# A two-layer attention encoder on one core: output shares at the handover from C to A, the turn of the output blocks, and the first load of x

## The chip, the cores and the metric

One core of a Trainium2 chip runs the whole program. The metric is the device time of one execution in microseconds (us); lower is better. The core has a matrix engine (PE, TensorE), three engines for elementwise work (DVE or VectorE, ACT or ScalarE, POOL or GpSimd), and a queue, SP, from which the transfers (DMA) are issued in order. Every engine works off its own list of instructions in order.

## What is computed

```python
for l in range(2):                                   # x: 1024 rows x 1024 features
    h = rms_norm(x, norm_g[l])
    aq, ak, av, ag, bq_lat, bkv_lat, bk_pe, bg, cq, ck, cv, cg = split_cols(h @ w_in[l])
    ya = dilated_attention(norm(aq), norm(ak), av) * silu(ag)     # 4 heads of 64
    yb = dense_attention(rope(norm(up(bq_lat))), ..., vb) * silu(bg)   # 6 heads, 96 wide
    yc = dense_attention(rope(norm(cq)), rope(norm(ck)), cv) * silu(cg)   # 6 heads, 2 for k and v
    x = x + concatenate([ya, yb, yc]) @ w_out[l]     # 256 + 384 + 384 features
```

## The kernel before, in words

Everything lies transposed: eight feature blocks of 128 partitions by 1024 positions. A matmul operand is split into a high part and a remainder, and a product takes three matmuls (high x high, high x remainder, remainder x high). `split` makes the parts: ACT writes the high part (L141), DVE or POOL the remainder (L145); `Stream` fetches weights over SP, splits them and hands them out in the order of `ws.add`. An engine given to `ws.add` fixes who makes the remainder; without one DVE and POOL take turns (`flip`).

The program begins with `WARM` 128-column matmuls on a tile of ones (L1327, each two matmul instructions of the trace). `bring` loads x chunk by chunk and prepares it (`x_prepare`: ACT L188, DVE L189; `x_square` adds up the squares, POOL L199). A layer then goes through the latent projection (L299 to L301, over k = 0..7), the v, q, kv, C and A projections, the gates (`gate(m)`, L657 to L659), six B heads and six C heads (dense), four A heads (dilated), and the output projection.

From the last four gates on, the order is a table of slots that is written by hand: `put(s, f, pri)` hangs a step on slot s, and `slots` runs them. A dense head takes 16 slots; the A heads begin around slot `base_a`. ACT keeps the order of the code; for PE, DVE, POOL and SP a scheduler sets the order from the code and the tiles' buffers. Row blocks m = 0..7 of the output take features k = 2, 3, 4 from B (`OF_B`), 5, 6, 7 from C (`OF_C`) and 0, 1 from A (`OF_A`). `EARLY[m]` says which of these are multiplied during the slots (`f_load` fetches the weights and splits them on POOL, L1087 and L1088; `f_load_x` fetches x; `f_mm` runs 9 matmuls of 512 columns for half a block, L1105 to L1107; `f_add` adds x, L1111, and stores to `x_part`), `LATE[m]` which come at the end. A block's sum lies in an S tile; there are two S tiles, and the score products (L748, L885 to L891) use them too. T tiles (four) take transposes.

An A head: score products `a_s` (L885 to L891), exponentials (L908, L910), a chain of small steps on DVE (`a_x1` to `a_x5`; `a_x4p` is a PE step, L965), then `a_norm_w` (L980) and `a_norm_c` (L984) scale the probabilities on POOL, and `a_t` transposes them on PE (L997, L1002) for the product with v (L1026). `a_end` (L1073) writes the result into the y tile of its feature block on ACT; `gate_load` (L799) loads the gate.

At the end of a layer (the output stage) `out_first` and `out_part` (L1251 to L1253) finish a block in an S tile, and `out_end` loads `x_part` (L1264), adds it (DVE L1265), stores x and, in the first layer, prepares the block for the next layer. A block that lacks only A's part is light here (12 matmuls), one that lacks C's and A's parts is heavy (30 matmuls).

## Time and profile before

| | |
|---|---|
| median of 3 runs | 1497.06 us (1496.88 to 1497.84) |
| the profiled execution | 1496.05 us, span 1494.3 us |
| PE busy | 1457.9 us (98%) |
| DVE, ACT, POOL busy | 1085.1 (73%), 895.9 (60%), 593.3 (40%) us |
| TensorE clock granted, mean | 0.991 of full |

The profile is of one execution; its own time is 1.01 us under the median, and 1.75 us of it lie outside the span. Busy time of PE includes matmuls that overlap the next one, so a PE at 100% may still run at half the clock.

### The profile page before, as it was taken

To read this page: it belongs to the slowest core of one execution; us is meant where nothing else is said; L and a number is where in the kernel's file an instruction comes from. 1 tells how busy PE (TensorE), PEld (TensorE's weight loads), DVE (VectorE), ACT (ScalarE), POOL (GpSimd) and SP (SyncE) were. 2 spreads that over 40 slices of the span, in tenths; PEclk is the share of its full clock that TensorE was granted. 3 is DMA by queue.
4 is the path that set the end of the run, shared out by engine and by line. 5 is a ranking of instruction groups with operands and counts; after the bars stand their busy time and mean duration, and the time that the engine had idled before them with its cause. 6 is when DMAs were issued, how large, how long until landed. Compare 5 with 4: busy or idle time off the path is not lost.

```text
span 1494.3 us, 23232 instructions
## 1 busy us (share of the span) xinstructions
PE 1457.9 (98%) x7928; PEld 1237.6 (83%) x7928; DVE 1085.1 (73%) x1994; ACT 895.9 (60%) x1667; POOL 593.3 (40%) x544
## 2 busy tenths in 40 slices
PE   9999999999999999899899999999999999998998
PEld 8998888788888888788679988888888888886887
DVE  6759757488889998564646497574888899985644
ACT  6572235388889997453324632343988899974531
POOL 6305421145456553553231044311354565535530
PEclk9999999999999999999999999999999999999999
DMA  7271146510342116742532621366103421157427
GB/s 229 74 249 41 51 153 200 160 57 29 91 122 57 29 43 188 202 149 80 177 131 66 242 60 50 115 208 190 57 29 79 121 69 31 43 170 208 140 72 249
DMA packets 119719, 176.01 MB, mean 118 GB/s; under 512 B 11696, under 2 KB 75568, under 8 KB 119600
## 3 DMA queue, kind: packets, MB, share of 16 engines
q1 hardware_dynamic: 119600, 174.52, 38.3%
q8 instruction: 63, 1.03, 0.3%
q14 instruction: 56, 0.46, 0.1%
HBM read 111.56 MB, written 62.91 MB: 117 GB/s over the span
## 4 chain that ended last, share of the span: by engine, by line
PE 90%; DVE 3%; issue 3%; ACT 2%; DMA 2%; POOL 1%; SPq 0%; ACTq 0%; DVEq 0%; POOLq 0%
PE S L748 15%; PE T L777 11%; PE acc L790 6%; PE acc L789 6%; PE T L658 4%; PE T L659 4%; PE T L657 4%; PE S L1105 2%; PE S L1106 2%; PE S L1107 2%; PE S L216 2%; PE S L217 2%; PE S L215 2%; PE T L693 1%; PE T L997 1%
## 5 line engine op out<-in xcount | busy, mean ns | idle before, releaser
L771 DVE TENSOR_TENSOR wl<-T,wh 128x512 fp32r<-128x512 f32 x440 | 297.6, 687 | 85.1 <-ACT wh L770 82.7
L770 ACT ACTIVATE wh<-T 128x512 fp32r<-128x512 f32 x440 | 261.1, 597 | 153.7 <-PE T L777 69.0
L764 POOL TENSOR_SCALAR u<-u,rec 128x1024 f32<-128x1024 f32 x192 | 216.8, 1129 | 272.5 <-DVE rec L763 155.2
L748 PE MATMUL S<-u,u 96*128 96x512 f32 (+1 forms) x960 | 269.2, 410 | 1.6 <-ACT u L757 1.3
L750 DVE TENSOR_REDUCE nmax<-S 128x1 f32<-128x1024 f32 x192 | 233.6, 1217 | 21.9 <-PE S L748 21.4
L777 PEld LDWEIGHTS T<-ident,u 128*128 128x128 f32 x1536 | 191.3, 140 | 50.3
L777 PE MATMUL T<-ident,u 128*128 128x128 f32 x1536 | 229.4, 272 | 0.0
L757 ACT ACTIVATE u<-S,nmax 128x1024 f32<-128x1024 f32 x192 | 213.2, 1111 | 0.3
L145 POOL TENSOR_TENSOR wl<-wr,wh 128x512 fp32r<-128x512 f32 (+2 forms) x48 | 77.6, 1619 | 318.0 <-ACT wh L141 307.2
L748 PEld LDWEIGHTS S<-u,u 96*128 96x128 f32 (+1 forms) x960 | 166.6, 189 | 29.7 <-ACT u L757 3.6
L141 ACT ACTIVATE wh<-wr 128x512 fp32r<-128x512 f32 (+2 forms) x96 | 56.8, 596 | 161.2 <-PE S L216 97.3
L657 PE MATMUL T<-u,wh 128*128 128x512 f32 x256 | 102.0, 399 | 0.0
L659 PE MATMUL T<-u,wl 128*128 128x512 f32 x256 | 100.1, 391 | 0.0
L658 PE MATMUL T<-u,wh 128*128 128x512 f32 x256 | 100.0, 391 | 0.0
L789 PE MATMUL acc<-wh,u 128*128 128x512 f32 x192 | 84.6, 441 | 0.0
L789 PE MATMUL acc<-wh,qb 128*128 128x512 f32 x192 | 82.8, 431 | 0.0
L790 PE MATMUL acc<-wl,u 128*128 128x512 f32 x192 | 75.9, 395 | 1.6 <-DVE wl L771 1.6
L790 PE MATMUL acc<-wl,qb 128*128 128x512 f32 x192 | 75.8, 395 | 0.0
L145 DVE TENSOR_TENSOR wl<-wr,wh 128x512 fp32r<-128x512 f32 (+2 forms) x48 | 42.3, 882 | 44.7 <-ACT wh L141 44.5
L1105 PE MATMUL S<-u,h 128*128 128x512 f32 x156 | 63.9, 409 | 1.6 <-DVE u L1111 1.6
L1107 PE MATMUL S<-u,h 128*128 128x512 f32 x156 | 61.7, 396 | 0.0
L1106 PE MATMUL S<-u,h 128*128 128x512 f32 x156 | 61.5, 394 | 0.0
(294 smaller groups left out, 3399.1 us busy)
## 6 DMA issues: line engine op xcount, KB each, us to landing
u<-qk_c SPq DMA_DIRECT2D x40, 256.0 KB, 4.4
wr<-in_w_g_dram SPq DMA_DIRECT2D x32, 256.0 KB, 2.6
gates<-h SPq DMA_DIRECT2D x32, 256.0 KB, 2.3
qk_c<-u SPq DMA_DIRECT2D x16, 512.0 KB, 4.0
u<-gates SPq DMA_DIRECT2D x16, 512.0 KB, 3.8
qb<-qk_a SPq DMA_DIRECT2D x32, 256.0 KB, 5.7
x_part<-u SPq DMA_DIRECT2D x16, 512.0 KB, 3.1
qb<-x_part SPq DMA_DIRECT2D x15, 512.0 KB, 4.2
```

Of the source, the lines that this page charges most:

```text
L657: T.matmul(ps[half], wh[:, w], xh[k][:, s], start=(k == 0), stop=False)
L658: T.matmul(ps[half], wh[:, w], xl[k][:, s], start=False, stop=False)
L659: T.matmul(ps[half], wl[:, w], xh[k][:, s], start=False, stop=(k == 7))
L748: T.matmul(ps[:, w], q[:, s], k[:, w], start=(i == 0), stop=(i == len(terms) - 1))
L750: V.tensor_reduce(nmax, ps, op=ALU.max, axis=AX.X, negate=True)
L757: A.activation(p, ps, AF.Exp, bias=nmax, accum_out=den)
L764: G.tensor_scalar(p, p, rec, 1.0, ALU.mult, ALU.mult)
L770: A.activation(ph, ps, AF.Copy)
L771: V.tensor_tensor(pl, ps, f32(ph), ALU.subtract)
L777: T.transpose(ps[:, i * P:(i + 1) * P], Pt[hd, 4 * half + i][0][:, j * P:(j + 1) * P], ident)
L789: T.matmul(acc, w, ph, start=(j == 0), stop=False)
L790: T.matmul(acc, w, pl, start=False, stop=(j == 7))
```

## The change

- `HALF_M`: blocks 0, 1, 3 and 5 have only B's part early, the others B's and C's. Before, blocks 0, 1 and 2 had. The four B shares stand four slots apart from `base_a - 10` on, so the last stands behind the handover; the shares of the other four blocks fill the A heads' slots (16 half blocks where 20 stood). One C share per layer, 18 matmuls, thereby goes from the A heads to the output stage.
- `f_load_x` is put three slots ahead of the block's last piece, where it was six slots ahead of its first.
- K, table and V of A's first head are put 40 and 36 slots ahead, where it was 6 to 8.
- In the output stage blocks 2 to 7 are now light, heavy, light, heavy, light, light; before heavy, then five light ones. The remainders of w_out's pieces go to DVE and POOL in turn; before those of m >= 2 went to DVE.
- `spread_r`, eight small products that spread the row norm r over the partitions (L641 to L645), is called inside `gate(0)` after k = 3; before it stood ahead of `gate(0)`.
- At the start x's chunk 0 is loaded and prepared in two halves, the first half first in SP's queue; the identity matrix goes to `load_tables`; `WARM` is 12 where it was 20; the first layer's k = 0 takes half 0 of all three row blocks ahead of half 1.

```diff
--- before.py
+++ after.py
@@ -25,8 +25,9 @@
 
 
 OF_B, OF_C, OF_A = (2, 3, 4), (5, 6, 7), (0, 1)
-EARLY = {m: ((OF_B,) if m < 3 else (OF_B, OF_C)) for m in range(8)}
-LATE = {m: ((OF_C, OF_A) if m < 3 else (OF_A,)) for m in range(8)}
+HALF_M = (0, 1, 3, 5)
+EARLY = {m: ((OF_B,) if m in HALF_M else (OF_B, OF_C)) for m in range(8)}
+LATE = {m: ((OF_C, OF_A) if m in HALF_M else (OF_A,)) for m in range(8)}
 
 
 @with_exitstack
@@ -87,7 +88,6 @@
         return ap.bitcast(F32)
 
     ident = cp.tile([P, P], F32, name="ident")
-    nc.sync.dma_start(ident, ident_in)
     ones = cp.tile([P, P], F32, name="ones")
     V.memset(ones, 1.0)
 
@@ -101,6 +101,7 @@
     sinb = cp.tile([P, NCH, 32], F32, name="sinb")
 
     def load_tables():
+        nc.sync.dma_start(ident, ident_in)
         nc.sync.dma_start(cosb, cosb_in)
         nc.sync.dma_start(sinb, sinb_in)
         nc.sync.dma_start(cosc, cosc_in)
@@ -183,10 +184,11 @@
     ws = Stream()
 
 
-    def x_prepare(k, x32, g_sb, xh, xl):
+    def x_prepare(k, x32, g_sb, xh, xl, parts=(slice(0, SEQ),)):
         hi, lo = U(F32R), U(F32R)
-        A.activation(hi, x32, AF.Copy, scale=g_sb[:, k:k + 1])
-        V.scalar_tensor_tensor(lo, x32, g_sb[:, k:k + 1], f32(hi), ALU.mult, ALU.subtract)
+        for s in parts:
+            A.activation(hi[:, s], x32[:, s], AF.Copy, scale=g_sb[:, k:k + 1])
+            V.scalar_tensor_tensor(lo[:, s], x32[:, s], g_sb[:, k:k + 1], f32(hi[:, s]), ALU.mult, ALU.subtract)
         xh.append(hi)
         xl.append(lo)
 
@@ -254,7 +256,7 @@
         g["c"] = gc
 
     state = {}
-    WARM, SK = 20, 3
+    WARM, SK = 12, 3
     MV = 2
     LS, UL = (2, 3, 4), (3, 4, 5)
     stores = []
@@ -291,14 +293,16 @@
                 load_tables()
             if k == 7:
                 make_gains2(g)
-            for m in range(3):
+            order = [(m, half) for m in range(3) for half in range(2)]
+            if k == 0 and l == 0:
+                order.sort(key=lambda e: e[1])
+            for m, half in order:
                 w = slice(m * P, m * P + P)
-                for half in range(2):
-                    o = bk[m][half]
-                    s = slice(half * 512, half * 512 + 512)
-                    T.matmul(o, wh[:, w], xh[k][:, s], start=(k == 0), stop=False)
-                    T.matmul(o, wh[:, w], xl[k][:, s], start=False, stop=False)
-                    T.matmul(o, wl[:, w], xh[k][:, s], start=False, stop=(k == 7))
+                o = bk[m][half]
+                s = slice(half * 512, half * 512 + 512)
+                T.matmul(o, wh[:, w], xh[k][:, s], start=(k == 0), stop=False)
+                T.matmul(o, wh[:, w], xl[k][:, s], start=False, stop=False)
+                T.matmul(o, wl[:, w], xh[k][:, s], start=False, stop=(k == 7))
         latr = [U() for _ in range(3)]
         for m in range(3):
             A.activation(latr[m][:, 0:512], bk[m][0], AF.Copy)
@@ -637,12 +641,14 @@
 
 
         r_bc = U()
-        ps = PS()
-        for c in range(NCH):
-            d = H()[:, :P]
-            V.tensor_scalar(d, ident, r[:, c:c + 1], None, ALU.mult)
-            T.matmul(ps[:, c * P:(c + 1) * P], ones, d, start=True, stop=True)
-        A.activation(r_bc, ps, AF.Copy)
+
+        def spread_r():
+            ps = PS()
+            for c in range(NCH):
+                d = H()[:, :P]
+                V.tensor_scalar(d, ident, r[:, c:c + 1], None, ALU.mult)
+                T.matmul(ps[:, c * P:(c + 1) * P], ones, d, start=True, stop=True)
+            A.activation(r_bc, ps, AF.Copy)
 
         last_u = []
 
@@ -658,6 +664,8 @@
                     T.matmul(ps[half], wh[:, w], xl[k][:, s], start=False, stop=False)
                     T.matmul(ps[half], wl[:, w], xh[k][:, s], start=False, stop=(k == 7))
                 run(0.8)
+                if m == 0 and k == 3:
+                    spread_r()
                 if hook is not None:
                     hook(m, k)
             for half in range(2):
@@ -1177,13 +1185,13 @@
                     put(base_a + AT0 + 8 * h + FA[1] + half, lambda h=h, half=half: fin_split(h // 2, half), 6)
         FP, FL = 6.5, 6
         rest = [(m, piece, half) for m in EARLY if len(EARLY[m]) > 1 for piece in range(2) for half in range(2)]
-        at = {(m, 0, half): base_a - 10 + 4 * m + half for m in EARLY if len(EARLY[m]) == 1 for half in range(2)}
+        at = {(m, 0, half): base_a - 10 + 4 * i + half for i, m in enumerate(HALF_M) for half in range(2)}
         at.update({u: base_a + 7 + 29 * i // len(rest) for i, u in enumerate(rest)})
         for (m, piece, half), s in at.items():
             if half == 0:
                 put(s - FL, lambda m=m, piece=piece: f_load(m, piece), 9)
-                if piece == 0:
-                    put(s - FL, lambda m=m: f_load_x(m), 9)
+                if piece == len(EARLY[m]) - 1:
+                    put(s - 3, lambda m=m: f_load_x(m), 9)
             put(s, lambda m=m, piece=piece, half=half: f_mm(m, piece, half), FP)
             if piece == len(EARLY[m]) - 1:
                 put(s + 1, lambda m=m, half=half: f_add(m, half), 6)
@@ -1205,9 +1213,10 @@
         for h in range(AH):
             s = a_slot(4 * h)
             put(s - 8, lambda h=h: q_load(qk_a, ("a", h), 0), 8)
-            put(s - 7, lambda h=h: k_load(qk_a, ("a", h), 2), 8)
-            put(s - 6, lambda h=h: a_load_tab(h), 8)
-            put(base_a + AT0 + 8 * h - 8, lambda h=h: a_load_v(h), 8)
+
+            put(s - (7 if h else 40), lambda h=h: k_load(qk_a, ("a", h), 2), 8)
+            put(s - (6 if h else 36), lambda h=h: a_load_tab(h), 8)
+            put(base_a + AT0 + 8 * h - (8 if h else 40), lambda h=h: a_load_v(h), 8)
 
         def slot(s):
             for _, _, f in sorted(at_slot.pop(s, []), key=lambda e: e[:2]):
@@ -1319,14 +1328,15 @@
         ws.hold()
         order = [(m, OF_C) for m in range(2)] + [(m, OF_A) for m in range(2)]
         for m, ks in order + [(m, ks) for m in range(2, 8) for ks in LATE[m]]:
-            ws.add(w_out[l, m, :, ks[0]:ks[-1] + 1, :], (P, len(ks), P), True, V if m >= MV else None)
+            ws.add(w_out[l, m, :, ks[0]:ks[-1] + 1, :], (P, len(ks), P), True, None)
 
 
     warm = PT()
     for _ in range(WARM):
         T.matmul(warm[:, :P], ones, ones, start=True, stop=True)
 
-    g = load_gains(0)
+    HALVES = (slice(0, 512), slice(512, SEQ))
+    g = {}
     xh, xl = [], []
     ss = QB()[:, :SEQ]
     loaded, done = [], [0]
@@ -1335,16 +1345,18 @@
         while len(loaded) < min(k + 3, 8):
             i = len(loaded)
             t = QB()[:, :SEQ]
-            nc.sync.dma_start(t, x_t[i * P:(i + 1) * P, :])
+            for j, s in enumerate(HALVES if i == 0 else (slice(0, SEQ),)):
+                nc.sync.dma_start(t[:, s], x_t[i * P:(i + 1) * P, s])
+                if i == 0 and j == 0:
+                    g.update(load_gains(0))
+                    ws.fetch(1)
             loaded.append(t)
 
     def bring(k):
-        if k == 0:
-            ws.fetch(1)
         x_load(k)
         while len(xh) < min(k + 2, 8):
             i = len(xh)
-            x_prepare(i, loaded[i], g["x"], xh, xl)
+            x_prepare(i, loaded[i], g["x"], xh, xl, HALVES if i == 0 else (slice(0, SEQ),))
         while done[0] < (k if k < 7 else 8):
             x_square(done[0], loaded[done[0]], ss)
             done[0] += 1
```

What the change moves in the engines' lists, at three places. Names end in a running number; h is a split weight of f_load, wr the raw one, qb and u operands.

PE before, the handover in the first layer: behind the last C products (L789, L790) come score products of A (L885 to L891), and among them the first transpose that needs POOL's L984 (L997).

```order
L789 MATMUL acc_6530<-wh_6681,qb_5314 128x512
L790 MATMUL acc_6530<-wl_6682,qb_5314 128x512
L885 MATMUL S_6754<-qb_6372,u_6342 128x256
L886 MATMUL S_6754<-qb_6373,u_6342 128x256
L890 MATMUL S_6754<-qb_6372,u_6345 128x256
L891 MATMUL S_6754<-qb_6373,u_6345 128x256
L885 MATMUL S_6754<-qb_6372,u_6342 128x192
L886 MATMUL S_6754<-qb_6373,u_6342 128x192
L890 MATMUL S_6754<-qb_6372,u_6345 128x256
L891 MATMUL S_6754<-qb_6373,u_6345 128x256
L885 MATMUL S_6793<-qb_6615,u_6594 128x192
L997 MATMUL T_6778<-ident,u_6329 128x128
```

The same place of PE after the change (L893 is a score product, L1113 to L1115 are f_mm):

```order
L797 MATMUL acc_6532<-wh_6682,qb_5309 128x512
L798 MATMUL acc_6532<-wl_6683,qb_5309 128x512
L1113 MATMUL S_6753<-u_3371,h_6598 128x512
L1114 MATMUL S_6753<-u_3372,h_6598 128x512
L1115 MATMUL S_6753<-u_3371,h_6599 128x512
L1113 MATMUL S_6753<-u_4066,h_6598 128x512
L1114 MATMUL S_6753<-u_4067,h_6598 128x512
L1115 MATMUL S_6753<-u_4066,h_6599 128x512
L1113 MATMUL S_6753<-u_4704,h_6598 128x512
L1114 MATMUL S_6753<-u_4705,h_6598 128x512
L1115 MATMUL S_6753<-u_4704,h_6599 128x512
L893 MATMUL S_6765<-qb_6374,u_6346 128x256
```

Nine matmuls of f_mm (the B share of block 5, first half, on tile S_6753) now follow the C products. Behind them come eight score products (the first, L893, is the last row shown), then nine more of f_mm, and only then the first transpose that needs the norms, L1005; before, nine score products alone stood ahead of it.

POOL before, the same place: the norms of the first head (L980, L984), with the split of a weight of f_load (L1087, L1088) between them.

```order
L980 TENSOR_SCALAR u_6456<-u_6456,sc_6705 128x256 x2
L980 TENSOR_SCALAR u_6517<-u_6517,sc_6705 128x256
L980 TENSOR_SCALAR u_6517<-u_6517,sc_6705 128x192
L1087 TENSOR_SCALAR h_6773<-wr_6772 128x384
L1088 TENSOR_TENSOR h_6774<-wr_6772,h_6773 128x384
L984 TENSOR_SCALAR u_6329<-u_6329,s2c_6744 128x256 x2
L984 TENSOR_SCALAR u_6402<-u_6402,s2c_6744 128x256 x2
```

POOL after (L988 and L992 are the norms, L1095 and L1096 the split):

```order
L988 TENSOR_SCALAR u_6460<-u_6460,sc_6708 128x256 x2
L988 TENSOR_SCALAR u_6519<-u_6519,sc_6708 128x256
L988 TENSOR_SCALAR u_6519<-u_6519,sc_6708 128x192
L1095 TENSOR_SCALAR h_6840<-wr_6839 128x384
L992 TENSOR_SCALAR u_6333<-u_6333,s2c_6745 128x256 x2
L992 TENSOR_SCALAR u_6404<-u_6404,s2c_6745 128x256 x2
L992 TENSOR_SCALAR u_6460<-u_6460,s2c_6745 128x256 x2
L818 TENSOR_TENSOR u_6121<-u_6121,u_6119 128x512
L1096 TENSOR_TENSOR h_6841<-wr_6839,h_6840 128x384
```

One instruction of the split, L1095, still stands ahead of the first L992; L1096 went behind the sixth.

DVE before, in the first layer's output stage: the add of a block's sum (L1265), the remainder of its preparation (L189), and the remainder of a weight piece (L145).

```order
L1265 TENSOR_TENSOR qb_8094<-S_8053,qb_8094 128x1024
L189 SCALAR_TENSOR_TENSOR u_8099<-qb_8094,gx_2692,u_8098 128x1024
L145 TENSOR_TENSOR qb_8107<-wr_8106,qb_8107 128x256
L1265 TENSOR_TENSOR qb_8123<-S_8105,qb_8123 128x1024
L189 SCALAR_TENSOR_TENSOR u_8128<-qb_8123,gx_2692,u_8127 128x1024
L145 TENSOR_TENSOR qb_8136<-wr_8135,qb_8136 128x256
L1265 TENSOR_TENSOR qb_8152<-S_8134,qb_8152 128x1024
L189 SCALAR_TENSOR_TENSOR u_8157<-qb_8152,gx_2692,u_8156 128x1024
L145 TENSOR_TENSOR wl_8166<-wr_8164,wh_8165 128x384
L1265 TENSOR_TENSOR qb_8182<-S_8163,qb_8182 128x1024
L189 SCALAR_TENSOR_TENSOR u_8187<-qb_8182,gx_2692,u_8186 128x1024
L1265 TENSOR_TENSOR qb_8212<-S_8193,qb_8212 128x1024
```

DVE after (L1274 the add, L191 the preparation, L146 the weight's remainder):

```order
L1274 TENSOR_TENSOR qb_8042<-S_8024,qb_8042 128x1024
L191 SCALAR_TENSOR_TENSOR u_8047<-qb_8042,gx_2687,u_8046 128x1024
L146 TENSOR_TENSOR qb_8055<-wr_8054,qb_8055 128x384
L1274 TENSOR_TENSOR qb_8094<-S_8053,qb_8094 128x1024
L191 SCALAR_TENSOR_TENSOR u_8099<-qb_8094,gx_2687,u_8098 128x1024
L146 TENSOR_TENSOR qb_8107<-wr_8106,qb_8107 128x256
L1274 TENSOR_TENSOR qb_8123<-S_8105,qb_8123 128x1024
L191 SCALAR_TENSOR_TENSOR u_8128<-qb_8123,gx_2687,u_8127 128x1024
L146 TENSOR_TENSOR wl_8160<-wr_8158,wh_8159 128x384
L1274 TENSOR_TENSOR qb_8176<-S_8134,qb_8176 128x1024
L191 SCALAR_TENSOR_TENSOR u_8181<-qb_8176,gx_2687,u_8180 128x1024
L1274 TENSOR_TENSOR qb_8206<-S_8187,qb_8206 128x1024
```

Three blocks still have a weight's remainder behind the preparation; the remainders of the other pieces went to POOL's list.

## Rows read from the trace of the kernel before

**Rows 1.** The page: span, and busy time of each engine.

```profile
span 1494.3 us, 23232 instructions
...
PE 1457.9 (98%) x7928; PEld 1237.6 (83%) x7928; DVE 1085.1 (73%) x1994; ACT 895.9 (60%) x1667; POOL 593.3 (40%) x544
```

**Rows 2.** Waits of PE: line, releaser, us in total, times, longest.

```profile
PE T L997 <- POOL u L984: 7.3, 3, 3.4
PE S L1251 <- DVE qb L1265: 7.2, 3, 3.2
PE S L644 <- DVE h L643: 1.7, 2, 0.8
PE S L885 <- DVE u L1111: 1.6, 2, 0.8
PE S L1105 <- DVE u L1111: 1.6, 2, 0.8
```

**Rows 3.** PE by stretch: length, busy (instructions), granted clock, DMA share, GB/s.

```profile
1.05:6.05 5.00, 5.00 (x23) 1.00 0.71 217
6.05:7.90 1.85, 1.85 (x19) 1.00 1.02 399
600.00:614.00 14.00, 10.58 (x58) 0.76 1.00 262
622.00:636.00 14.00, 10.42 (x67) 1.00 0.48 151
715.00:728.00 13.00, 13.00 (x58) 1.00 0.41 144
728.00:790.00 62.00, 51.12 (x194) 0.89 0.45 148
1350.00:1362.00 12.00, 8.56 (x53) 0.86 1.01 265
1371.00:1386.00 15.00, 11.93 (x68) 0.89 0.53 164
```

**Rows 4.** Timeline of the handover in the first layer, POOL and PE: start, length.

```profile
602.26 3.56 POOL L980 TENSOR_SCALAR u<-u,sc 128x192 f32<-128x192 f32 x8 [3.18 <-DVE sc L954]
...
605.78 0.52 POOL L1087 TENSOR_SCALAR h<-wr 128x384 fp32r<-128x384 f32 x1
...
606.39 1.00 POOL L1088 TENSOR_TENSOR h<-wr,h 128x384 fp32r<-128x384 f32 x1
...
607.90 0.47 PE L997 MATMUL T<-ident,u 128*128 128x128 f32 x1 [3.42 <-POOL u L984]
```

**Rows 5.** Waits of ACT between 600 and 640 us.

```profile
ACT u L1073 <- PE S L886: 11.0, 1, 11.0
```

**Rows 6.** Timeline of one light block in the first layer's output stage.

```profile
736.95 1.21 DVE L1265 TENSOR_TENSOR qb<-S,qb 128x1024 f32<-128x1024 f32 x1
...
738.20 1.15 ACT L188 ACTIVATE u<-qb,gx 128x1024 fp32r<-128x1024 f32 x1 [3.74 <-DVE qb L1265]
...
739.38 1.28 DVE L189 SCALAR_TENSOR_TENSOR u<-qb,gx,u 128x1024 fp32r<-128x1024 f32 x1 [1.22 <-ACT u L188]
...
740.44 2.44 POOL L199 TENSOR_TENSOR qb<-qb,qb 128x1024 f32<-128x1024 f32 x1 [3.69 <-ACT qb L198]
740.63 2.53 DVE L145 TENSOR_TENSOR qb<-wr,qb 128x256 fp32r<-128x256 f32 x1
743.09 1.21 DVE L1265 TENSOR_TENSOR qb<-S,qb 128x1024 f32<-128x1024 f32 x1
```

**Rows 7.** Timeline of the start.

```profile
4.59 0.56 DVE L145 TENSOR_TENSOR wl<-wr,wh 128x384 fp32r<-128x384 f32 x1 [3.26 <-ACT wh L141]
...
7.92 1.17 PE L299 MATMUL T<-u,wh 128*128 128x512 f32 x4
...
9.75 1.54 ACT L141 ACTIVATE wh<-wr 128x384 fp32r<-128x384 f32 x3 [0.67 <-DMA wr<-in_w_lat_dram]
...
10.36 2.31 POOL L145 TENSOR_TENSOR wl<-wr,wh 128x384 fp32r<-128x384 f32 x2 [9.92 <-ACT wh L141]
...
12.13 0.39 PE L299 MATMUL T<-u,wh 128*128 128x512 f32 x1
12.36 0.39 PE L300 MATMUL T<-u,wh 128*128 128x512 f32 x1
12.58 0.39 PE L301 MATMUL T<-u,wl 128*128 128x512 f32 x1
```

## The prediction

> **What bounds the kernel now.** I read the page first: of a span of 1494.3 us PE is busy for 1457.9, and no other engine comes near [rows 1]. So what PE does is the bound nearly everywhere, and a change that takes no matmuls away can only win back the time in which PE waits or runs at its lower clock. The second view is the list of PE's waits. It names few: 7.3 us for the norm L984, 7.2 us for the block add L1265, 1.7 us for the spread of r (L643), and 1.6 us each for score products and f_mm that wait for f_add to free an S tile [rows 2]. Third, the stretches say what each wait costs with its consequences. Without a gap 58 matmuls of 512 columns start in 13.00 us, 0.224 us each; the distances of single starts are 0.23 [rows 3, 7]. In 728 to 790 there are 194 in 62.00 us, which at 0.227 would need 44.0: 18.0 us are lost in the first layer's output stage. The granted clock there is 0.89 on average, so part of the loss is time at 1.2 GHz, not waiting. At the handover from C to A, 600 to 614 holds 3.4 us without a matmul and a granted clock of 0.76 (14 x 0.24 = 3.4 us lost if PE had work); 622 to 636 holds 3.6 us idle. The second layer repeats it: 3.4 us idle and 12 x 0.14 = 1.7 us of clock, then 3.1 idle and 15 x 0.11 = 1.7 of clock [rows 3].
>
> **The start.** PE's first real matmul comes at 7.92 us behind 40 warm-up matmuls [rows 7]. These start every 0.217 us before 6.05 us (23 in 5.00) and every 0.10 after it (19 in 1.85); the clock column has 1.00 there, so the halving is read from the distances alone [rows 3]. With 24 of them the warm-up ends at about 6.1 us, and the first half of chunk 0 should be prepared by then, as it is first in the queue and half as long. That is 1.8 us earlier. But the product L301 of k = 1 needs the remainder of the second weight, which comes from POOL: it starts at 10.36 and makes two in 2.31, so the first is there at about 11.5 [rows 7]. The transfers ahead of that weight are nearly the same ones as before. L301 of k = 1 ran at 12.58, so not more than 1.1 us can be won before the weight is the limit. I take 1.1; bounds 0 (x's half comes late) and 2.1 (the weight lands sooner without the identity ahead of it).
>
> **The spread of r.** Its wait, 1.7 us over two layers [rows 2], goes if the eight products stand inside a gate in which PE has work. They still run, and the copy out of the S tile by ACT is wanted much later. I take 1.7; bounds 0 and 2.0.
>
> **The handover.** PE waited until 607.90 for the first L984, which stood on POOL behind L980 (3.56 us from 602.26) and the split L1087 and L1088 (0.52 and 1.00) [rows 4]. Now 18 matmuls of f_mm lie ahead of that transpose, 18 x 0.227 = 4.1 us of work against a wait of 3.42, and L1088 is behind the norms, which makes them 1.0 us earlier. So this wait should be gone, and the drop of the clock behind it too. The second wait comes from ACT, which stood for 11.0 us in front of one copy, L1073 [rows 5]: its y tile took a buffer that a score product had to read first. Meanwhile PE's f_mm halves ran back to back and waited for f_add on their S tile. In the new order the y tile's buffer is released by an early POOL step, and other work stands between the two halves of a block. Idle time 3.4 + 3.6 + 3.4 + 3.1 = 13.5 us and clock 3.4 + 1.7 + 1.7 = 6.8 us make 20.3 for both layers. What is late next is an S tile: score products behind the new f_mm block reuse the tile that f_add has to empty, and such a wait is 0.8 us now (1.6 for two) [rows 2]. I leave two of these in each layer, 3.2 us, and take 17.1. Bounds: 0 and 20.3. K, table and V of A's first head were in place long before their use and are not what PE waited for, so their earlier load is worth nothing; the work that covers it is the C heads. The C share that leaves the A heads (18 matmuls, 4.1 us per layer) is done in the output stage, at the same price in both places as long as PE is the bound in both.
>
> **The first layer's output stage.** A light block has 12 matmuls, 2.7 us. But the blocks followed one another every 6.14 us (L1265 at 736.95 and 743.09): the add 1.21, ACT's high part 1.15, the remainder L189 1.28, and then the weight's remainder L145, which took 2.53 beside POOL's L199 of 2.44, though a longer one took 0.56 with POOL idle [rows 6, 7]. With two S tiles PE can run only two blocks ahead, so it waited for L1265. In the new turn a pair of a light and a heavy block brings PE 42 x 0.227 = 9.5 us. DVE needs for a pair two adds, two L189 and one slow L145: 2 x 2.49 + 2.53 = 7.5 us. PE is then the bound again. The pair light, light at the end has the first 9 matmuls of the next layer's projection between its blocks. What remains: a light block's `x_part` load is issued behind that block's own last matmul, and the first of the projection's weights come in while POOL adds squares. I leave 4.5 us of the 18.0 and take 13.5; bounds 4.5 (the chain of 6.1 us stays for three of the blocks) and 18. Moving weight remainders to POOL costs POOL 1.15 each (2.31 for two [rows 7]); it was idle 3.69 us ahead of each square add [rows 6].
>
> The Trainium skill, in SBUF — State Buffer (section "SBUF: two separate sides"), says that a DVE instruction with two SBUF inputs and a POOL instruction lock a shared port pair against each other for their whole length. By that L189, which has two such inputs, could be held up by a POOL remainder where before there was none; the trace shows only the case of L145 and L199. With four remainders moved the sum would be up to 4 x 1.15 = 4.6 us worse, an estimate from the row of POOL's remainder; it stands below as a rival.
>
> **The sum.** 1.1 + 1.7 + 17.1 + 13.5 = 33.4 us. The profiled execution took 1496.05, so 1462.7; it lies 1.0 under the median of the runs, so the forecast for a median is 1463.7, in round figures **1464 us**.
>
> **The rivals.**
> (a) *The handover keeps half its wait.* If a block's x from `f_load_x`, now issued three slots ahead instead of six, or an f_mm weight lands late, PE waits for about the same length in another place. For it: the transfers ran at full share in 600 to 614 and 1350 to 1362 (1.00 and 1.01) [rows 3]. Against it: the loads of the first blocks are issued in the C heads. It gives 1464 + 8.5 = 1472.5.
> (b) *The output stage stays bound by the blocks' chain*, with a wait of 1 to 2 us at each of six blocks. For it: the chain add, high part, remainder alone is 3.64 us, and `x_part` has to be stored and loaded ahead of it. Against it: 9.5 against 7.5 us for a pair. With half of the 13.5 us it gives 1471.
> (c) *POOL's remainders hold up L189.* 1464 + 4.6 = 1468.6; for it speaks 2.53 beside 2.44 us [rows 6], against it that a pair has 2 us to spare.
> (d) *The shorter warm-up leaves the first products at 1.2 GHz.* If the clock rises only after the first 18 products (they take 4.1 us at the full rate, twice that at half), PE is past k = 0 at 14.2 instead of 12.13: 1.1 us won become 2.1 lost, 1467. The Trainium skill, in TensorE: Matmul & The Clock Gate (Part 1), says that the slow state is the default and that sustained work releases it, which speaks against a shorter warm-up; in this trace the distances halved at 6.05 us, while only warm-up had run.
> (e) *Slower than before: the weights of f_mm come late at every share.* Place: POOL's L1087 and L1088 in the C and A heads. There are 12 f_load per layer, 24 in all. Behind a run of norms (3.56 us) each could be late. From 33.4 / 24 = 1.4 us of PE wait each, the whole gain is gone; at 2.0 us the time is 1464 + 48 = 1512. Against it: before there were 13 per layer on the same path, and PE's f_mm never waited for a weight, only for S tiles (1.6 us) [rows 2].
> (f) *No effect*: the waits only change places, and the time stays at 1497.
>
> **How the numbers follow.** Forecast 0.55, and by its own terms 1459 to 1470 us; (a) 0.14, (b) 0.14, (c) 0.05, (d) 0.04, (e) 0.04, (f) 0.04. Lower end of the range: all bounds at their best, 2.1 + 2.0 + 20.3 + 18.0 = 42.4, 1496.05 - 42.4 + 1.0 = 1455; I take 1456. Upper end: (a) and (b) together, 1464 + 8.5 + 6.75 = 1479, with (d) 1482. A change of under 0.2%, about 3 us, can hardly be told from none. Only (e) is slower by more: 0.04; within it (f) and a piece of (e), 0.04; faster 0.92.
>
> **What would show it.** In the changed profile the wait for the norms (L992 in the new line numbers) and the one for the block add (L1274) should be gone from the list of PE's waits or be under 2 us each; the clock should stay at 2.4 GHz between 600 and 640, 720 and 790, and 1345 and 1390; ACT should not stand for more than a few us in front of a_end's copy; the spread's products should show no wait; the first L301 of k = 1 should come at about 11.5 us. The prediction is wrong if PE waits for f_mm weights or x in the A heads, if the granted clock in the output stage is again near 0.89, or if the A heads, with 18 matmuls fewer, no longer keep PE full.

## The result, and the profile after

The change makes the kernel faster: 1477.16 us (median of 4 runs, 1475.67 to 1478.02) against 1496.97 us (4 runs), ratio 0.9867 with a 95% interval of 0.9850 to 0.9884. That is 19.8 us of the 33.4 that were forecast; the time lies in the whole range of 1456 to 1482, near its upper end, but 13 us above the forecast and outside the 1459 to 1470 that the forecast's own terms allowed.

The starts of the first and last matmul of each stage in the two traces say where (in us from the span's start). "Won" is the length of the stretch before minus after; the sum is 19.7.

| stretch ends with | before | after | won |
|---|---|---|---|
| last product of the first latent projection | 40.46 | 40.67 | -0.2 |
| last gate product, first layer | 295.66 | 294.16 | 1.7 |
| last score product of B and C | 569.83 | 568.22 | 0.1 |
| first out_part (handover and A heads) | 703.54 | 690.04 | 11.9 |
| last product of the next latent projection (output stage) | 791.25 | 780.29 | -2.5 |
| last gate product, second layer | 1044.85 | 1033.10 | 0.8 |
| last score product | 1319.02 | 1307.18 | 0.1 |
| first out_part | 1453.16 | 1429.02 | 12.3 |
| last matmul | 1489.76 | 1470.10 | -4.5 |

The 18 matmuls that moved from the A heads to the output stage are 4.1 us in each layer. Without them the handover won 7.8 and 8.2 us, the first layer's output stage 1.6 us, and the second layer's lost 0.4.

PE's list of waits after the change (line, releaser, us in total, times, longest):

```profile
PE S L1260 <- DVE qb L1274: 4.5, 2, 2.6
PE T L305 <- POOL wl L146: 3.3, 2, 2.3
PE S L1113 <- DVE u L1119: 1.7, 2, 0.9
...
PE S L650 <- DVE h L649: 0.4, 2, 0.2
```

The wait for the norms, 7.3 us before [rows 2], is not in it any more, and the spread's products wait 0.4 instead of 1.7. The wait for the block add fell only from 7.2 to 4.5. By stretch (start and end, length, PE busy, granted clock, DMA share, GB/s):

```profile
600.00:618.00 18.00, 17.98 (x112) 1.00 0.96 261
618.00:640.00 22.00, 20.36 (x142) 1.00 0.82 247
704.00:728.00 24.00, 19.49 (x72) 0.88 0.52 183
742.00:765.00 23.00, 17.60 (x67) 0.93 0.43 145
1340.00:1357.00 17.00, 16.98 (x105) 1.00 0.96 266
1357.00:1380.00 23.00, 21.36 (x151) 1.00 0.78 243
```

The handover is full and at 2.4 GHz in both layers; what is left there is 1.6 us idle per layer. The norms come early enough for the first transpose, which starts without a wait, and no wait of ACT for a_end's copy (now L1081), 11.0 us before [rows 5], is left in 600 to 640:

```profile
604.69 2.76 POOL L992 TENSOR_SCALAR u<-u,s2c 128x256 f32<-128x256 f32 x6
...
606.94 0.60 PE L1005 MATMUL T<-ident,u 128*128 128x128 f32 x4
```

The output stage is not full: it has waits and a granted clock of 0.88 again. There the timeline shows something that the prediction had not priced:

```profile
706.41 0.33 SPq L1276 DMA_DIRECT2D x_scr<-qb  x1
...
706.78 0.42 SPq L1273 DMA_DIRECT2D qb<-x_part  x1
...
710.72 1.23 DVE L1274 TENSOR_TENSOR qb<-S,qb 128x1024 f32<-128x1024 f32 x1 [1.83 <-DMA qb<-x_part]
711.97 0.32 SPq L1276 DMA_DIRECT2D x_scr<-qb  x1
...
712.09 0.77 PE L1260 MATMUL S<-u,qb 128*128 128x512 f32 x1 [2.62 <-DVE qb L1274]
...
712.33 0.43 SPq L1273 DMA_DIRECT2D qb<-x_part  x1
...
717.65 1.23 DVE L1274 TENSOR_TENSOR qb<-S,qb 128x1024 f32<-128x1024 f32 x1 [3.21 <-DMA qb<-x_part]
```

Read it as a ring. SP issues the store of a block (L1276) when the block's add is done, and only behind it the load of the next block's x_part (L1273). The load lands 3.9 to 5.3 us later, the next add takes 1.23, then comes the next store. One turn takes 5.6 and 6.9 us in these rows, and PE and DVE wait for it. Of the eight adds of the stage five wait for x_part in this way; DVE's own list of waits says it in one line:

```profile
DVE qb L1274 <- DMA qb<-x_part: 10.4, 5, 3.9
```

### The profile page after: what moved, and what is told of

Same layout as the page of the kernel before. It is cut to its first block, busy times and chain, and to the rows that moved or that the text cites. A ratio compares the mean times of both kernels' runs of the same rounds, so it can differ in the third digit from the quotient of the medians.

```text
span 1474.6 us, 23206 instructions
## 1 busy us (share of the span) xinstructions
PE 1450.3 (98%) x7912; PEld 1229.9 (83%) x7912; DVE 1086.3 (74%) x1989; ACT 897.1 (61%) x1670; POOL 599.6 (41%) x548
## 4 chain that ended last, share of the span: by engine, by line
PE 92%; DVE 3%; DMA 2%; ACT 1%; issue 1%; SPq 0%; POOL 0%; ACTq 0%; DVEq 0%; POOLq 0%
PE S L756 15%; PE T L785 11%; PE acc L798 6%; PE acc L797 6%; PE T L663 4%; PE T L664 4%; PE T L665 4%; PE S L1113 2%; PE S L1115 2%; PE S L1114 2%; PE S L218 2%; PE S L217 2%; PE S L219 2%; DMA qb<-x_part 2%; PE T L701 1%
## 5 line engine op out<-in xcount | busy, mean ns | idle before, releaser
L146 POOL TENSOR_TENSOR wl<-wr,wh 128x512 fp32r<-128x512 f32 (+2 forms) x48 | 74.7, 1561 | 316.7 <-ACT wh L142 307.2
L146 DVE TENSOR_TENSOR wl<-wr,wh 128x512 fp32r<-128x512 f32 (+2 forms) x48 | 44.8, 933 | 39.6 <-ACT wh L142 39.5
L1113 PE MATMUL S<-u,h 128*128 128x512 f32 x144 | 59.0, 410 | 1.7 <-DVE u L1119 1.7
L1115 PE MATMUL S<-u,h 128*128 128x512 f32 x144 | 57.0, 396 | 0.0
L1114 PE MATMUL S<-u,h 128*128 128x512 f32 x144 | 57.0, 396 | 0.0
```

## The theories and the experiments

**Theory Q**: the blocks of the first layer's output stage are paced by this ring through SP. **Rival R**: they are paced by add, high part and remainder on DVE and ACT, with POOL's square add in the way of DVE, and the transfer is only next to it. For the rest: is the handover's gain due to the spread shares, to the later x or to the earlier loads of A's first head; and what did the start win?

Ratios are against the kernel before, run beside it on the same chip. "Stage" is the first layer's output stage, from the first out_part to the last product of the next latent projection; it is 87.7 us before and 90.3 after the change, 4.1 of it moved work.

| kernel | time, us | ratio (95%) | stage, us |
|---|---|---|---|
| the change | 1477.16 | 0.9867 (0.9850 to 0.9884) | 90.3 |
| e1 x_part ahead | 1464.83 | 0.9779 (0.9764 to 0.9794) | 78.5 |
| e7 no x_part load | 1461.0, one run | | 74.2 |
| e9 before, x_part ahead | 1489.97 | 0.9937 (0.9919 to 0.9954) | 80.6, without the moved work |
| e10 ahead, remainders on DVE | 1467.23 | 0.9784 (0.9769 to 0.9799) | 80.7 |
| e14 ahead, remainders on POOL | 1461.38 | 0.9756 (0.9741 to 0.9770) | 75.5 |
| e11 the change, heavy 0, 1, 2, 3 | 1479.03 | 0.9864 (0.9846 to 0.9882) | 91.1 |
| e12 ahead, heavy 0, 1, 2, 3 | 1465.23 | 0.9778 (0.9762 to 0.9794) | 78.3 |
| e2 before, shares alone | 1479.29 | 0.9872 (0.9854 to 0.9890) | 90.1 |
| e4 the change, old first loads | 1476.25 | 0.9854 (0.9839 to 0.9870) | 89.4 |
| e15 the change, x early | 1482.69, one run | | 90.4 |
| e8 ahead, old start | 1465.96 | 0.9777 (0.9762 to 0.9793) | 78.8 |

### e1 and e7: is it the ring?

```diff
+        def load_part(m):
+            ahead[m] = [H(), H()]
+            for half in range(2):
+                nc.sync.dma_start(ahead[m][half], x_part[m * P:(m + 1) * P, half * 512:half * 512 + 512])
...
         def out_end(m, ps):
             xr = QB()[:, :SEQ]
-            nc.sync.dma_start(xr, x_part[m * P:(m + 1) * P, :])
-            V.tensor_tensor(xr, ps, xr, ALU.add)
+            if l + 1 < DEPTH:
+                for half in range(2):
+                    s = slice(half * 512, half * 512 + 512)
+                    V.tensor_tensor(xr[:, s], ps[:, s], ahead[m][half], ALU.add)
+                if m + 3 < 8:
+                    load_part(m + 3)
+            else:
+                nc.sync.dma_start(xr, x_part[m * P:(m + 1) * P, :])
+                V.tensor_tensor(xr, ps, xr, ALU.add)
...
         slots(end + 1)
+        if l + 1 < DEPTH:
+            for m in range(3):
+                load_part(m)
```

> The changed kernel, but in the first layer's output stage x_part is loaded up to three blocks ahead into spare tiles, two halves each, so that the load no longer stands in SP's queue behind the store of the block before. Theory Q (the blocks are paced by SP: the load of a block is issued only after the store of the one before, which waits for that block's add; about 4 us to landing, 1.2 for the add, 0.4 of issue): the wait of the add for x_part (10.4 us, 5 times) goes, PE's waits for the add (4.5 us) go with it and the clock stays up; output stage 8 to 11 us shorter, total 1466 to 1469. Theory R (the blocks are paced by the chain add, high part, remainder and by POOL's square add blocking DVE): the adds still follow one another every 6 us; total 1474 to 1477, since two half adds cost 0.2 us more per block.

Measured: 1464.83 us, 0.9779, 12 us faster than the change; the stage is 11.8 us shorter. This is what Q said, and a little more. The stretch from 690 to 760, PE alone, first of the change and then of e1:

```profile
690.00:760.00 70.00, 59.95 (x244) 0.95 0.48 164
```

```profile
690.00:760.00 70.00, 66.06 (x288) 1.00 0.49 165
```

44 more matmuls start in the same 70 us, and the clock stays at 2.4 GHz. DVE's wait of the add for x_part is gone from its list. The edit also makes each add in two halves; the next run has the add whole.

The second run takes the load away altogether; the add uses a resident tile, so the residual and the early shares are left out of the sum:

```diff
             xr = QB()[:, :SEQ]
-            nc.sync.dma_start(xr, x_part[m * P:(m + 1) * P, :])
-            V.tensor_tensor(xr, ps, xr, ALU.add)
+            if l + 1 < DEPTH:
+                V.tensor_tensor(xr, ps, f32(yh[0]), ALU.add)
```

> The changed kernel, but in the first layer's output stage x_part is not loaded at all: the add takes a tile that is resident anyway (this leaves the residual and the early shares out of the sum). Theory Q: like the run with the loads ahead or a little better, 1465 to 1469, adds every 5 us or less where PE has a block ready. Theory R: 1474 to 1477.

Measured: 1461.0 us in one run, stage 74.2. R is refuted as the main cause: the chain on DVE, ACT and POOL is all still there, with the whole add, and the stage is 16 us shorter. It is also 4.3 us shorter than in e1, and why loading ahead doesn't give back as much as leaving the load away was not tried.

### e9: was the ring there before the change?

The edit of e1 in the kernel before.

> The kernel before with x_part loaded ahead in the first layer's output stage, nothing else. In its profile the add waited for a transfer only twice (3.5 us); mostly it followed straight behind a weight's remainder on DVE (L145, 2.53 us beside POOL's square add). If DVE and POOL paced its blocks and SP's loop stood just behind: 1 to 5 us gained, total 1492 to 1496. If SP's loop paced them there too: 10 us or more gained, 1487 or less.

Measured: 0.9937, 9.4 us by the ratio; the stage is 7.1 us shorter (80.6 against 87.7). This lies between the two expectations, and above what I had said for "the ring just behind". The order that makes the ring was there before the change, the load of a block behind the store of the block before in SP's queue:

```profile
725.54 0.32 SPq L1267 DMA_DIRECT2D x_scr<-qb  x1
725.91 0.43 SPq L1264 DMA_DIRECT2D qb<-x_part  x1
```

Yet DVE's list of the kernel before showed little of it:

```profile
DVE qb L1265 <- DMA qb<-x_part: 3.5, 2, 2.1
```

Four of the eight adds came straight behind a slow remainder L145, and such an add shows no wait for x_part, since DVE's waits list names only what came last. The two limits stood near each other: 6.14 us between adds [rows 6], 5.6 and more for the ring in the change. That e9 won more than the 3.5 us fits this but isn't shown to come from it, because the edit also halves the add, and DVE now puts a weight's remainder between the halves, where it takes 1.98 us and not 2.53:

```profile
734.34 0.68 DVE L1274 TENSOR_TENSOR qb<-S,h 128x512 f32<-128x512 f32 x1
734.94 1.98 DVE L145 TENSOR_TENSOR qb<-wr,qb 128x256 fp32r<-128x256 f32 x1
736.85 0.68 DVE L1274 TENSOR_TENSOR qb<-S,h 128x512 f32<-128x512 f32 x1
```

The loads ahead and the halves were not tried apart in the kernel before.

### e10 and e14: what are the remainders' places worth once the ring is gone?

e10 is e1 with

```diff
-            ws.add(w_out[l, m, :, ks[0]:ks[-1] + 1, :], (P, len(ks), P), True, None)
+            ws.add(w_out[l, m, :, ks[0]:ks[-1] + 1, :], (P, len(ks), P), True, V if m >= MV else None)
```

and e14 is e1 with

```diff
-            ws.add(w_out[l, m, :, ks[0]:ks[-1] + 1, :], (P, len(ks), P), True, None)
+            ws.add(w_out[l, m, :, ks[0]:ks[-1] + 1, :], (P, len(ks), P), True, G if m >= MV else None)
```

> The changed kernel with x_part loaded ahead (1464.8 us), and the weight remainders of blocks 2 to 7 on DVE again. If POOL's share of them is worth something once the loop through SP is gone, five more remainders of up to 2.5 us stand on DVE and PE waits for the add again: 1468 to 1475. If the turn of heavy and light blocks alone is enough: 1464 to 1467.

> The changed kernel with x_part loaded ahead, and all weight remainders of blocks 2 to 7 on POOL. They take 2.0 to 2.8 us on DVE beside POOL's square add and 1.0 to 1.1 on POOL. If DVE's slow remainders are what is left of PE's waits for the add (2.9 us): those waits under 1 us, 1462 to 1465. If POOL then holds up DVE's L191 (1.28 us, once 2.99 beside POOL) or its own list gets late: 1466 to 1470.

Measured against e1's stage of 78.5: 80.7 with the remainders on DVE, 75.5 with all of them on POOL. The first costs 2.2 us of stage; by the ratios (0.9784 and 0.9779) e10 and e1 can't be told apart, and its 1467.23 us lie between the two outcomes. The second wins 3.0 and is the fastest kernel of the study that leaves nothing out, 1461.38 us, 0.9756. With the ring in place the remainders' places made no such difference: e2, which has them on DVE and no loads ahead, needs 90.1 us for the stage, the change 90.3. In e14 PE's waits for the add are gone from its list, and the same stretch reads:

```profile
690.00:760.00 70.00, 68.90 (x303) 1.00 0.48 163
```

Its timeline also prices the rival that POOL's remainders hold up DVE (L191 takes 1.28 us alone):

```profile
718.08 1.74 POOL L146 TENSOR_TENSOR qb<-wr,qb 128x384 fp32r<-128x384 f32 x2
719.17 1.73 DVE L191 SCALAR_TENSOR_TENSOR u<-qb,gx,u 128x1024 fp32r<-128x1024 f32 x1 [1.22 <-ACT u L190]
```

L191 began while POOL worked on a remainder and took 0.45 us longer than alone; in e1 one L191 beside POOL's square add took 2.99:

```profile
738.14 2.39 POOL L201 TENSOR_TENSOR qb<-qb,qb 128x1024 f32<-128x1024 f32 x1
738.63 2.99 DVE L191 SCALAR_TENSOR_TENSOR u<-qb,gx,u 128x1024 fp32r<-128x1024 f32 x1
```

The Trainium skill, SBUF — State Buffer (section "SBUF: two separate sides"), says that a DVE instruction with two inputs in SBUF and a POOL instruction that reads SBUF lock each other out for a whole instruction. These rows agree with it: in both L191 ends 1.1 us after POOL has ended, near its own length of 1.28.

### e11 and e12: is the turn of heavy and light blocks worth anything?

```diff
-HALF_M = (0, 1, 3, 5)
+HALF_M = (0, 1, 2, 3)
```

> The changed kernel (no loads ahead) with blocks 0, 1, 2 and 3 as those without C's early share: the shares at the handover stay where they are, but the output stage is heavy, heavy, then four light ones. Theory Q: the blocks follow one another every 6.3 to 7 us through SP whatever PE has to do, so the turn is worth little: 1475 to 1481. If the turn is what brought the stage its time: 1483 or more.

> The changed kernel with x_part loaded ahead (1464.8 us; its first layer's output stage, from the first out_part to the last product of the next latent projection, is 78.5 us), and blocks 0, 1, 2, 3 as the heavy ones, so that four light blocks follow one another. If the turn counts once the loop through SP is gone: a light block gives PE 2.7 us, DVE needs some 5 for it with a weight's remainder; PE waits 2 us at three blocks and the clock falls, stage 83 us or more, total 1469 to 1475. If the loop was all: stage within 1.5 us of 78.5, total 1464 to 1467.

Measured: 0.9864 against 0.9867 without the loads ahead, 0.9778 against 0.9779 with them; the stages are 91.1 against 90.3 and 78.3 against 78.5. The turn is worth nothing that can be measured in either case. For e11 that is what Q said. For e12 the first of the two outcomes, 83 us or more, was not met and the other one was: with x_part loaded up to three blocks ahead, four light blocks in a row do not stop PE for an add; that wait is not in its list.

### e2, e15 and e4: what removed the handover's waits?

e2 is the kernel before with HALF_M, the four slots of the shares and the later f_load_x, nothing else.

> The kernel before with only the new places of the output shares: HALF_M and with it the turn of heavy and light blocks, the shares' slots, f_load_x later. Start, spread of r, engines of the weight remainders and first loads of A as before. If the handover's gain is due to the spread shares alone: handover and A heads 11 to 12 us shorter in each layer, of which 4.1 come back in the output stage; first layer's output stage as in the changed kernel or up to 3 us longer; total 1479 to 1483. If the earlier first loads of A take part in it: total above 1487.

Measured: 1479.29 us, 0.9872; from the last score product to the first out_part 121.7 and 121.8 us (133.7 and 134.1 before, 121.8 in the change). The whole gain of the handover is in these edits.

e4 puts only the first loads of A back:

```diff
-            put(s - (7 if h else 40), lambda h=h: k_load(qk_a, ("a", h), 2), 8)
-            put(s - (6 if h else 36), lambda h=h: a_load_tab(h), 8)
-            put(base_a + AT0 + 8 * h - (8 if h else 40), lambda h=h: a_load_v(h), 8)
+            put(s - 7, lambda h=h: k_load(qk_a, ("a", h), 2), 8)
+            put(s - 6, lambda h=h: a_load_tab(h), 8)
+            put(base_a + AT0 + 8 * h - 8, lambda h=h: a_load_v(h), 8)
```

> The changed kernel with K, table and V of A's first head put at the old slots. If the earlier load is worth nothing, as forecast: within 1 us of the changed kernel, 1476 to 1478. If it is what removed the wait at the handover: 1482 or more, with PE waiting for a transfer or for POOL near 604 and 1344 us.

Measured: 1476.25 us, 0.9854. The earlier loads are worth nothing, as forecast. e15 puts only f_load_x back:

```diff
-                if piece == len(EARLY[m]) - 1:
-                    put(s - 3, lambda m=m: f_load_x(m), 9)
+                if piece == 0:
+                    put(s - FL, lambda m=m: f_load_x(m), 9)
```

> The changed kernel with f_load_x at its old place, six slots ahead of a block's first piece. If the later load of x takes part in removing the second wait of the handover (tiles are taken in another turn, so that ACT's copy L1081 waits again for a score product): the stretch from 618 to 640 us has 2 us more of idle time than the changed kernel and ACT stands there for 5 us or more; both layers together 4 us or more. If the spread of the shares alone did it: the same as the changed kernel, within 1 us in each layer.

Measured: 1482.69 us in one run. From the last score product to the first out_part it takes 124.1 and 125.3 us, 2.3 and 3.4 more than the change. The place was not the one that I had named: the first wait of the handover is back, in both layers (PE's waits over the whole span, then SP's and ACT's around 600 to 640):

```profile
PE T L1005 <- POOL u L992: 5.8, 2, 2.9
```

```profile
SPq L1101 <- PE S L899: 4.7, 1, 4.7
```

```profile
ACT u L1081 <- PE T L1010: 4.8, 1, 4.8
```

ACT stands in front of its copy again, for 4.8 us, and SP for 4.7 us in front of a load of x whose tile a score product still has to read. But neither is what brought PE's wait back: in the first layer the copy comes at 623.21 and that load at 630.84, long after the transpose at 608.59, and the change, which keeps the whole gain, has such a wait of SP too:

```profile
SPq L1101 <- PE T L1010: 4.9, 1, 4.9
```

By stretch PE's loss is in 600 to 618 (17.98 us busy in the change), not in 618 to 640:

```profile
600.00:618.00 18.00, 15.06 (x96) 1.00 0.75 220
618.00:640.00 22.00, 20.79 (x141) 1.00 0.81 236
```

What the rows show in its place is another order. Behind the last product of C, PE's list has nine products of f_mm and eight score products ahead of the first transpose, and only then the other nine; in the change all 18 stand ahead of it. POOL also begins the norms 2.0 us later, counted from the last score product of B and C (34.4 us behind it against 32.4):

```profile
603.20 1.34 POOL L988 TENSOR_SCALAR u<-u,sc 128x192 f32<-128x192 f32 x3 [4.28 <-DVE sc L962]
...
608.59 0.33 PE L1005 MATMUL T<-ident,u 128*128 128x128 f32 x1 [2.91 <-POOL u L992]
```

So about 5.7 of the handover's 16.0 us hang on the late load of x, and the rest on the other edits of e2; this is one run. That the load's place acts through the order of PE's and DVE's lists is read from these rows; why the scheduler chose another order was not followed.

### e8: the start

e1 with the old start.

> The changed kernel with x_part loaded ahead (1464.8 us) and the start of the kernel before (20 warm-up products, x's first chunk in one piece, the identity first). If the new start is worth nothing, since its second half waits for ACT and the second weight lands no earlier: 1464 to 1465.5, with k = 7 done at about 40.5 us in both. If it is worth the forecast 1.1 us: 1466 or more.

Measured: 1465.96 us, between the two outcomes; by the ratios, 0.9777 and 0.9779, e8 and e1 can't be told apart. The traces say more. In the stretch that was meant, the first latent projection, the new start is worth nothing that can be seen: its last product starts at 40.73 in e8 and 40.91 in e1, and over all traces at 40.44 to 40.76 with the old start (four, mean 40.60) and at 39.50 to 41.08 with the new one (nine, mean 40.37). In the change's timeline one sees why:

```profile
5.79 0.71 PE L303 MATMUL T<-u,wh 128*128 128x512 f32 x2
...
7.37 0.72 ACT L190 ACTIVATE u<-qb,gx 128x512 fp32r<-128x512 f32 x1 [1.85 <-DMA qb<-in_x_t_dram]
...
8.14 0.50 PE L303 MATMUL T<-u,wh 128*128 128x512 f32 x1 [1.40 <-ACT u L190]
...
8.71 0.39 PE L305 MATMUL T<-u,wl 128*128 128x512 f32 x1
...
8.94 0.39 PE L304 MATMUL T<-u,wh 128*128 128x512 f32 x1
...
10.44 1.51 ACT L142 ACTIVATE wh<-wr 128x384 fp32r<-128x384 f32 x3 [0.68 <-DMA wr<-in_w_lat_dram]
...
12.12 0.50 PE L305 MATMUL T<-u,wl 128*128 128x512 f32 x1
```

The first product comes 2.1 us earlier (5.79 against 7.92), but the second half of x lands late enough to stop PE for 1.4 us, and the second weight reaches ACT at 10.44, where it was 9.75 before [rows 7]. L305 of k = 1 runs at 12.12, not at 11.5.

But by the last gate product e8 is 1.3 us behind e1 (295.49 against 294.23), in one wait of PE in the first B head. First e8, then e1:

```profile
PE S L754 <- ACT u L763: 1.6, 1, 1.6
```

```profile
PE S L756 <- ACT u L765: 0.3, 1, 0.3
```

ACT's exponential comes behind work of DVE, and DVE stands in both kernels for a transfer of 0.5 KB, the next layer's gains of A, which SP issued at 272.84 in e8 and at 273.24 in e1. It is released at:

```profile
277.94 0.15 DVE L248 TENSOR_SCALAR gaq<-ga 128x1 f32<-128x1 f32 x1 [9.46 <-DMA ga<-in_a_g_dram]
```

```profile
276.67 0.15 DVE L248 TENSOR_SCALAR gaq<-ga 128x1 f32<-128x1 f32 x1 [8.12 <-DMA ga<-in_a_g_dram]
```

From the first issue to this step it takes 4.7 to 5.2 us in the four kernels with the old start and 3.4 to 3.9 in the nine with the new one; PE's wait is 1.3 to 2.0 us in the four and at most 0.6 in the nine. So the new start does go with some 1.3 us, 240 us behind the place that was meant. Why the transfer lands earlier isn't shown.

## Why the prediction came out as it did

- **The output stage** is the step that failed: 13.5 us forecast, 1.6 won. In the words of the prediction, "DVE needs for a pair two adds, two L189 and one slow L145 ... 7.5 us. PE is then the bound again." The 7.5 us are only DVE's work. The sign of being wrong that the prediction named for this stage, a granted clock near 0.89, came: 0.88 in 704 to 728. The blocks also hang on SP, where the load of a block's x_part stands behind the store of the block before. That ring needs 5.6 to 6.9 us per block, 12 or more for a pair, against PE's 9.5. I had named the load as issued behind the block's own last matmul; in the trace it was issued behind the store. Rival (b) had the right place and the right symptom ("x_part has to be stored and loaded ahead of it"), but was given 0.14 and half the loss. With the ring taken out (e1) the stage is 9.2 us shorter than before with 4.1 us more work in it, 13.3 in all, near the forecast's 13.5, and 16.3 in e14: the stage held what was forecast, but the ring had to go for it. The turn of heavy and light blocks, on which my argument stood, was worth nothing that could be measured (e11, e12).
- **The handover**: 17.1 forecast, 16.0 measured (7.8 and 8.2). Right in size and for the reason given for the first wait: counted from the last score product, POOL begins the norms L992 1.1 us earlier and PE comes to the transpose 4.1 us later, which is the time of the 18 products, and the clock does not fall. Of "two of these in each layer", 1.6 us left, the size is right, 1.6 us idle per layer, but only one wait for f_add per layer, 0.9 us at most, is of the kind named. What I had costed at nothing, the later load of x, carries 5.7 us of it, through the order of the lists (e15).
- **The spread of r**: 1.7 forecast; the wait fell from 1.7 to 0.4, so 1.3. The gates stretch won 1.7 and 0.8; of the first, 1.3 us is the wait of the first B head for ACT, which goes with the start and not with the spread of r (e8).
- **The start**: 1.1 forecast, -0.2 measured in the latent projection. The step that failed is "the transfers ahead of that weight are nearly the same ones as before", from which it was to be ready at 11.5 as it had been; it came 0.7 us later. The 1.3 us that go with the new start at the first B head, in no term of the prediction, make up for it: that the start is worth about 1.1 us in all is luck. Rival (d), the clock, did not happen: PE's distances in the first products are 0.23 us (8.71 and 8.94 above), as at the full rate before.
- **The earlier loads of A's first head**: nothing, as forecast (e4).
- **The other rivals**: (a) half the handover's wait stays: no. (c) POOL's remainders hold up L189: it happens, 0.35 to 0.45 us each in e14, which is a third of the price I gave it, and less than moving them wins. (e) late weights of f_mm: no such wait in PE's list. (f) no effect: no, the interval lies below 1.

The best kernel that the study led to is e14: the change, x_part loaded up to three blocks ahead, and the remainders of blocks 2 to 7 on POOL: 1461.38 us, 0.9756 (0.9741 to 0.9770), which is 36 us under the kernel before and 16 under the change.

## What to carry to other kernels

When a stage is paced by a loop, add up every resource that the loop passes, the queue included: a load that stands in an in-order queue behind a store that waits for the previous result closes a ring of its own, and a list of waits hides it wherever another limit ends last. Take such a limit out alone (load ahead, or leave the load away) before you rearrange work around it. And a long wait in a list isn't yet a cause: compare it with the same list of the faster kernel, and look whether it lies ahead of the loss in time (e15).

## What the runs showed of the hardware that was not expected

- A list of waits can show less than a limit is worth: 3.5 us of waits for x_part before the change, in a stage that became 7.1 us shorter with the loads ahead and the adds halved (e9).
- The same 0.5 KB transfer reached DVE 3.4 to 3.9 us behind its issue in nine kernels and 4.7 to 5.2 us in four, by the order of the transfers at the start, 270 us earlier (e8); why isn't shown.
- DVE's L191 can more than double beside POOL: 2.99 us once beside a square add, against 1.28 alone. Before the change only L145 had shown this.
